# Projection om of a gated attention and mLSTM layer: eight block products, or seven by Strassen's identity

## The chip, the cores and the metric

The kernel runs on one core of one Trainium2 chip. The metric is the device time of one execution in microseconds; the median of several runs is given. The core has five engines with queues of their own: TensorE (PE in the profile, its weight loads PEld), VectorE (DVE), ScalarE (ACT), GpSimd (POOL) and SyncE (SP), which here issues most DMA transfers. They are ordered only by semaphores.

## The reference

One layer over 256 tokens of width 1024, in float32. A normalised and modulated h (256 x 1024) is multiplied by one wide weight matrix, and the product is cut into projections:

```python
h = _rmsnorm(x, norm_w) * (1 + scale) + shift          # scale, shift, gate from c @ w_ada
(qa, ka, va, za, qm, km, vm, zm, om, ig, fg, ga, gm) = jnp.split(h @ w_in, SPLIT_IDX, axis=-1)
ya = (attention(rmsnorm(qa), rmsnorm(ka), va) * silu(za)) @ w_att_proj
hm = mlstm(silu(conv(qm)), silu(conv(km)), vm, ig, fg)  # 4 heads of 256
hm = sigmoid(om) * hm
ym = (rmsnorm_per_head(hm) * silu(zm)) @ w_ml_proj
y = sigmoid(ga) * ya + sigmoid(gm) * ym
return x + gate * (y @ w_out)
```

Each of the wide projections is 256 x 1024 times 1024 x 1024. The change concerns `h @ w_in[:, om]`, of which only the sigmoid is used, and only in the mLSTM output.

## The kernel before, in words

**Precision.** Matrices are multiplied in a fast float32 form that keeps part of the mantissa. To keep float32 accuracy each operand is split into a high part and the rest, and a product takes three matmuls: high by high, high by rest, rest by high. h is split once into `hTh` and `hTl`, both transposed (8 k-tiles of 128 rows, 256 tokens). The weights are split as they pass: `split(g)` copies a weight group to `wh` on ACT (line 448) and subtracts to get `wl` on DVE (line 452; on POOL for the few groups in `pool_lo`).

**Groups.** After a first phase (modulation, and projections qa and ka by `mm_row`, line 198), the rest is a list of `chunks`, half a projection each, in a fixed order: va (three chunks), za, qm, km, att, zm, vm, om, ga, gm, ml, out (two each). A chunk of 512 output columns is four *groups*, each with two k-tiles of weights. The main loop runs over groups g. Projections of kind `tok` (zm, vm, om, out) hold tokens on the output partitions: per group 2 k-tiles x 2 token halves x 3 = 12 matmuls of 512 columns (lines 999 to 1001). Projections of kind `ws` hold the weights still: 24 matmuls of 256 columns (lines 1006 to 1009).

**The split ring.** `wh` and `wl` have five buffers (`HB = 5`). At step g the loop first issues `split(g + 4)`, which reuses the buffers of group g - 1; then, at the first group of a chunk, the evacuation of the chunk before (`EV`: `ev_vm` line 706, `ev_om` line 712, `ev_ga` line 718 and others); then the *hooks* of that step (`at(step, fn)`), an order of the other work written out by hand; then the group's matmuls. Every engine works its queue in this order.

**Weight loads.** SP loads weights in 1 MB pieces to six `raw` buffers (line 376): a piece holds two k-tiles of both halves of a projection, and `pump` issues the load six pieces on when a piece has been split for the last time. The weights of the modulation gate (`ada_gate`) come as four more 1 MB pieces ahead of the projections in `GSEG`, and are summed on DVE by `gate_acc` (line 832), two at a time, four and three groups ahead of that projection.

**PSUM.** Two large tiles `mm` (two banks each) alternate between chunks; four small tiles `aux` serve everything else.

**Around om.** With groups counted from va, zm is 44 to 51, vm 52 to 59, om 60 to 67, ga 68 to 75, gm 76 to 83, ml 84 to 91. `ml_scores` (lines 757 to 768) runs during zm and into vm. `ml_num` (lines 779 to 786) makes a head's nine matmuls, multiplies by sigmoid(om) on DVE (783) and sums squares on ACT; `ml_y` normalises two heads on DVE, POOL and DVE (line 805); `ml_T` transposes on PE (816) and splits the result (820, 821) for projection ml. For heads 0 and 1 these hang on the end of om's first half (steps 65, 66, 67, then 71, 72), for heads 2 and 3 on the end of its second half (69, 70, 71, then 75, 76).

**Slots.** Large tiles share tagged memory slots: a new tile in a slot waits for all accesses of the one before.

Of the kernel before, what the change touches and what calls it, by code (L numbers as in the profile page):

```python
# [9 lines left out]
F32 = mybir.dt.float32  # L10
# [5 lines left out]
D = 1024  # L16
# [50 lines left out]
def tile_hybrid(ctx: ExitStack, tc: tile.TileContext, x, c, params2, w_row, w_va, ada_mod, ada_gate,  # L67
# [304 lines left out]
    def mk_pair(src, c0, kp):  # L372
# [68 lines left out]
    def split(g, between=()):  # L441
        li, ks, cs = raw_of[g]
        w = rawt[li][:, ks, cs]
        n = chunks[g // 4]["n"]
        at0 = WS_AT if chunks[g // 4]["kind"] == "ws" else 0
        h = hl.tile([128, RING], F32R, name="wh", bufs=HB)[:, at0:at0 + 1024].rearrange("p (k n) -> p k n", k=2)[:, :, 0:n]
        l = hl.tile([128, RING], F32R, name="wl", bufs=HB)[:, at0:at0 + 1024].rearrange("p (k n) -> p k n", k=2)[:, :, 0:n]
        nc.scalar.copy(h, w)  # L448
# [3 lines left out]
        e.tensor_tensor(l, w, h.bitcast(F32), op=OP.subtract)  # L452
        whl[g] = (h, l)
# [252 lines left out]
        nc.scalar.copy(T["vm"][:, :, hs, 0:MD], v)  # L706
        nc.vector.tensor_tensor(T["vml"][:, :, hs], v, T["vm"][:, :, hs, 0:MD].bitcast(F32), op=OP.subtract)

    def ev_om(pt, half):
        if half == 0:  # L710
            T["om"] = slot("s2", [128, 2, D], F32, "omt")
        nc.scalar.activation(T["om"][:, :, half * 512:half * 512 + 512], pt, AF.Sigmoid)
# [135 lines left out]

    def gate_columns(kp):

        li, ks, cs = raw_of[4 * C["out", 1] + kp]
        w = rawt[li][:, ks, cs]
        nc.gpsimd.tensor_tensor(w, w, T["gateb"][:, cs].unsqueeze(1).to_broadcast([128, 2, 512]), op=OP.mult)

    def ev_out(pt, c0, n, t):
        cs = slice(c0, c0 + n)
        o = hl.tile([128, n], F32, name="o", tag="scr", bufs=2)
        if c0 < 512:
# [49 lines left out]
    at(4 * C["att", 0] - 10, gate_init)  # L908
    gate_left = {}
    for q, nm in enumerate(GSEG):  # L910
        s = 4 * C[nm, 0] - 4
        at(s, gate_acc, 2 * q)
        at(s + 1, gate_acc, 2 * q + 1)
        gate_left[s + 1] = gate_loads[q]
    at(4 * C["ga", 0], gate_write)
    at(4 * C["gm", 0] + 4, gate_read)
    for q in range(4):
        at(4 * C["ml", 0] + 3 + q, gate_columns, q)
    for hp in range(2):
# [28 lines left out]
        consumed.update(li for li in cons.get(g, []) if li not in gate_loads)  # L948
    pump()
    for g in range(NG):  # L950
        ci, kp = divmod(g, 4)
        ch = chunks[ci]
        if g + A < NG:
            split(g + A, hooks_between.get(g, []))
            consumed.update(li for li in cons.get(g + A, []) if li not in gate_loads)
        if kp == 0:
            if ci > 0:
                pc = chunks[ci - 1]
                if pc["name"] in EV and ci - 1 != C["za", 0]:
# [5 lines left out]
            if ci < NCH - 1:  # L965
# [12 lines left out]
        sh_, sl_ = (hTh, hTl) if ch["stat"] is None else (T[stat[ch["stat"]][0]], T[stat[ch["stat"]][1]])  # L978
        wh, wl = whl[g]
        if ci == NCH - 1:  # L980
            continue
        for kk in range(2):
            k = 2 * kp + kk
            first, last = k == 0, k == KT - 1
            if ch["name"] == "out":

                for i in (0, 1):
                    for t, c0 in ((0, 0), (0, 256), (1, 0), (1, 256)):
                        a = (sh_, sl_)[i][:, k, t * 128:(t + 1) * 128]
                        cs = slice(c0, c0 + 256)  # L990
                        for w in (wh, wl)[:2 - i]:
                            nc.tensor.matmul(mmt[ci][:, t, cs], a, w[:, kk, cs],  # L992
                                             start=first and i == 0 and c0 == 0 and w is wh,
                                             stop=last and i == 1 and c0 > 0, skip_group_check=True)
            elif ch["kind"] == "tok":
                for t in range(2):
                    a, b = sh_[:, k, t * 128:(t + 1) * 128], sl_[:, k, t * 128:(t + 1) * 128]
                    o = mmt[ci][:, t]
                    nc.tensor.matmul(o, a, wh[:, kk], start=first, stop=False)  # L999
                    nc.tensor.matmul(o, a, wl[:, kk], start=False, stop=False)  # L1000
                    nc.tensor.matmul(o, b, wh[:, kk], start=False, stop=last)  # L1001
            else:
                for i in range(4):
                    cs = slice(i * 128, (i + 1) * 128)
                    o = mmt[ci][:, i]
                    nc.tensor.matmul(o, wh[:, kk, cs], sh_[:, k], start=first and i % 2 == 0, stop=False,  # L1006
                                     skip_group_check=True)
                    nc.tensor.matmul(o, wh[:, kk, cs], sl_[:, k], start=False, stop=False, skip_group_check=True)  # L1008
                    nc.tensor.matmul(o, wl[:, kk, cs], sh_[:, k], start=False, stop=last and i % 2 == 1,  # L1009
                                     skip_group_check=True)  # L1010
    ci = NCH - 1
    for t, c0, n in ((0, 0, 512), (1, 0, 256), (1, 256, 256)):
        pt = ps.tile([128, n], F32, name="mm", bufs=2)
# [62 lines left out]
```

## Time and profile before

| | |
|---|---|
| median of 3 runs | 351.48 us (351.32, 351.48, 351.49) |
| profiled execution: first to last instruction (span) | 350.0 us |
| PE busy | 344.3 us, 98% |
| DVE, ACT, POOL busy | 247.0, 213.3, 87.8 us |
| DMA moved | 77.79 MB, mean 222 GB/s |
| TensorE clock granted | full |

The profiled execution is given by its span; the time of an execution on the device, as the runs list it, has some work around the span as well. Rows of a timeline read: start, duration, engine, line, operation, output <- inputs, shape, count, and in brackets how long the engine sat idle before and what released it. Rows of a group: line, engine, operation, count | busy us, mean ns | idle before and its releaser. The duration of a matmul contains its way through the array, so matmuls overlap: the distance of two starts is what counts. Rows of the windows give for each engine the busy time and, in brackets, the instructions.

### The profile page before, as it was taken

How to read it: one execution, taken by the hardware profiler on the slowest of the kernel's cores; microseconds unless marked ns; L12 is line 12 of the kernel's file. 1: busy time of each engine (PE TensorE's matmuls, PEld its weight loads, DVE VectorE, ACT ScalarE, POOL GpSimd, SP SyncE). 2: the span in 40 equal slices, each digit the busy share in tenths (PEclk: the TensorE clock that was granted, in tenths of full speed). 3: DMA queues.
4: the chain of work that ended last, by engine and by line, in shares of the span. 5: the costliest groups of instructions: out<-in, count | busy, mean ns of one | idle time of the engine just before them, and what ended most of it. 6: DMA issues, size and time to landing. Idle time of an engine off the chain costs nothing.

```text
span 350.0 us, 6175 instructions
## 1 busy us (share of the span) xinstructions
PE 344.3 (98%) x2432; PEld 323.1 (92%) x2432; DVE 247.0 (71%) x369; ACT 213.3 (61%) x331; POOL 87.8 (25%) x81
## 2 busy tenths in 40 slices
PE   8999999999999999999999999999999999999996
PEld 7788889999999999999998888888899999999995
DVE  4999996976994437768866693864475775469961
ACT  4768779799777867675646554445646374543510
POOL 4400002942202462555004352000010320452000
PEclk9999999999999999999999999999999999999999
DMA  7999999890671554493874837659119129291011
GB/s 286 416 413 416 415 419 418 223 385 13 197 285 62 161 200 134 151 375 125 322 279 151 330 120 245 237 163 388 51 29 381 72 70 367 107 292 69 2 62 60
DMA packets 23517, 77.79 MB, mean 222 GB/s; under 512 B 3001, under 2 KB 4929, under 8 KB 22849
## 3 DMA queue, kind: packets, MB, share of 16 engines
q1 hardware_dynamic: 23336, 76.87, 59.9%
q10 hardware_dynamic: 152, 0.53, 0.5%
q8 instruction: 19, 0.31, 0.3%
q14 instruction: 10, 0.07, 0.1%
HBM read 76.14 MB, written 1.25 MB: 221 GB/s over the span
## 4 chain that ended last, share of the span: by engine, by line
PE 96%; DMA 2%; DVE 1%; issue 0%; SPq 0%; ACT 0%; DVEq 0%; ACTq 0%
PE mm L1009 15%; PE mm L1006 15%; PE mm L1008 15%; PE pm L198 13%; PE mm L999 8%; PE mm L1000 8%; PE mm L1001 8%; PE mm L992 3%; DMA adat<-in_ada_mod_dram 2%; PE mm L1021 1%; PE aux L642 1%; PE mm L1020 1%; PE mm L1019 1%; PE aux L492 1%; PE aux L604 1%; PE aux L762 1%
## 5 line engine op out<-in xcount | busy, mean ns | idle before, releaser
L452 DVE TENSOR_TENSOR wl<-raw,wh 128x1024 fp32r<-128x1024 f32 (+1 forms) x92 | 118.7, 1302 | 64.1 <-ACT wh L448 64.1
L448 ACT CAST wh<-raw 128x1024 fp32r<-128x1024 f32 (+1 forms) x100 | 100.5, 1015 | 54.2 <-PE mm L1001 26.7
L1006 PE MATMUL mm<-hTh,wh 128*128 128x256 f32 x320 | 90.0, 281 | 0.0
L1008 PE MATMUL mm<-hTl,wh 128*128 128x256 f32 x320 | 88.7, 277 | 0.0
L1009 PE MATMUL mm<-hTh,wl 128*128 128x256 f32 x320 | 88.7, 277 | 0.0
L1006 PEld LDWEIGHTS mm<-hTh,wh 128*128 128x128 f32 x320 | 60.2, 188 | 0.0
L1008 PEld LDWEIGHTS mm<-hTl,wh 128*128 128x128 f32 x320 | 60.2, 188 | 0.0
L1009 PEld LDWEIGHTS mm<-hTh,wl 128*128 128x128 f32 x320 | 60.1, 188 | 0.0
L999 PE MATMUL mm<-wh,hTh 128*128 128x512 f32 (+1 forms) x144 | 53.0, 368 | 0.0
L1000 PE MATMUL mm<-wl,hTh 128*128 128x512 f32 (+1 forms) x144 | 52.6, 365 | 0.0
L1001 PE MATMUL mm<-wh,hTl 128*128 128x512 f32 (+1 forms) x144 | 52.6, 365 | 0.0
L1001 PEld LDWEIGHTS mm<-wh,hTl 128*128 128x128 f32 x144 | 27.0, 188 | 3.8
L999 PEld LDWEIGHTS mm<-wh,hTh 128*128 128x128 f32 x144 | 27.0, 188 | 3.6
L1000 PEld LDWEIGHTS mm<-wl,hTh 128*128 128x128 f32 x144 | 27.1, 188 | 3.5
L452 POOL TENSOR_TENSOR wl<-raw,wh 128x1024 fp32r<-128x1024 f32 x8 | 19.5, 2461 | 18.4 <-ACT wh L448 12.1
L183 ACT CAST wrh<-raw 128x512 fp32r<-128x512 f32 (+1 forms) x24 | 18.2, 761 | 8.0 <-DMA raw<-in_w_row_dram 7.9
L188 DVE TENSOR_TENSOR wrl<-raw,wrh 128x512 fp32r<-128x512 f32 (+1 forms) x26 | 20.3, 807 | 0.5 <-ACT wrh L183 0.5
L198 PE MATMUL pm<-wrh,hTh 128*128 128x512 f32 x64 | 19.9, 392 | 0.8 <-ACT hTh L168 0.8
L198 PE MATMUL pm<-wrh,hTl 128*128 128x512 f32 x64 | 19.8, 391 | 0.0
L198 PE MATMUL pm<-wrl,hTh 128*128 128x512 f32 x64 | 18.7, 391 | 0.0
L1009 PE MATMUL mm<-yah,wl 128*128 128x256 f32 x64 | 17.7, 276 | 0.0
L1006 PE MATMUL mm<-yah,wh 128*128 128x256 f32 x64 | 17.7, 276 | 0.0
(218 smaller groups left out, 659.3 us busy)
## 6 DMA issues: line engine op xcount, KB each, us to landing
raw<-in_w_in_dram SPq DMA_DIRECT2D x32, 1024.0 KB, 5.2
adat<-in_ada_mod_dram SPq DMA_DIRECT2D x16, 512.0 KB, 8.8
raw<-in_w_va_dram SPq DMA_DIRECT2D x6, 688.0 KB, 9.2
raw<-in_ada_gate_dram SPq DMA_DIRECT2D x4, 1024.0 KB, 6.8
raw<-in_w_att_proj_dram SPq DMA_DIRECT2D x4, 1024.0 KB, 4.8
raw<-in_w_ml_proj_dram SPq DMA_DIRECT2D x4, 1024.0 KB, 6.3
raw<-in_w_out_dram SPq DMA_DIRECT2D x4, 1024.0 KB, 6.3
raw<-in_w_row_dram SPq DMA_DIRECT2D x15, 256.0 KB, 8.1
```

What stands on the lines that cost most here:

```text
L183: copy(wsp[k][0][:, c0:c1], wrow[k][:, c0:c1])
L188: e.tensor_tensor(l[:, cs], wrow[k][:, cs], h[:, cs].bitcast(F32), op=OP.subtract)
L198: nc.tensor.matmul(pm[ch][:, t], a[:, k, t * 128:(t + 1) * 128], b[:, cs], start=k == 0 and i == 0, stop=k == KT - 1 and i == 2)
L448: nc.scalar.copy(h, w)
L452: e.tensor_tensor(l, w, h.bitcast(F32), op=OP.subtract)
L992: nc.tensor.matmul(mmt[ci][:, t, cs], a, w[:, kk, cs], start=first and i == 0 and c0 == 0 and w is wh, stop=last and i == 1 and c0 > 0, sk ...
L999: nc.tensor.matmul(o, a, wh[:, kk], start=first, stop=False)
L1000: nc.tensor.matmul(o, a, wl[:, kk], start=False, stop=False)
L1001: nc.tensor.matmul(o, b, wh[:, kk], start=False, stop=last)
L1006: nc.tensor.matmul(o, wh[:, kk, cs], sh_[:, k], start=first and i % 2 == 0, stop=False, skip_group_check=True)
L1008: nc.tensor.matmul(o, wh[:, kk, cs], sl_[:, k], start=False, stop=False, skip_group_check=True)
L1009: nc.tensor.matmul(o, wl[:, kk, cs], sh_[:, k], start=False, stop=last and i % 2 == 1, skip_group_check=True)
```

## The change

om is written as a 2 x 2 block product: tokens in two halves of 128, k in two halves of 512, columns in two halves of 512. Instead of eight block products, seven are made (`OM_PRODUCTS`, Strassen's identity in Winograd's form). A block product is a chunk of kind `sums` with two groups, each of 2 k-tiles x 3 = 6 matmuls of 512 columns, so om is 14 groups (60 to 73), ga starts at 74, gm at 82, ml at 90. Each product has a weight block of its own, a 1 MB load: three blocks of `w_in`, and four sums of blocks.

- The four sums of weight blocks are made in DRAM by eight DMAs that POOL issues, four plain copies and four that add, at steps 10, 15, ... 45.
- The four sums of blocks of h are made on DVE at steps 53 to 57 (`h_full`, `h_sum`), each split on ACT and DVE.
- The products go to four small `aux` tiles in place of the large ones. Products 0 and 2 use the first, 1 and 3 the second, 4 and 6 the third, 5 the fourth; the second of a pair is added to the first in PSUM after the first has been read. `ev_om(j)` runs at the first group after product j: on ACT for j = 0 and 2, on DVE for 1 and 3, on DVE and then a sigmoid on ACT for 4, 5, 6.
- `ml_num`, `ml_y` and `ml_T` of heads 0 and 1 hang on the end of om (75, 76, 77, then 81, 82), those of heads 2 and 3 three groups later (78, 79, 80, then 84, 85).
- The gate loads and `gate_acc` move one projection ahead (`GSEG`), since a slot that they use now holds a sum of h.

```diff
+OM_PRODUCTS = (((0, 0), 0), (1, 1), ((1, 0), 0), (2, 1), (0, 2), (3, 3), ((1, 1), 2))
+OM_FIRST = (0, 1, 4, 5)
+OM_SUMS = ((0, (0, 0), False), (2, (0, 1), False), (0, (0, 1), True), (2, (1, 1), True),
+           (1, 0, False), (1, (1, 1), True), (3, 1, False), (3, (1, 0), True))
+OM_SUM_AT = 10
...
-    seg("tok", win, COL["om"], "om")
+    for j, (blk, bank) in enumerate(OM_PRODUCTS):
+        chunks.append(dict(kind="sums", blk=blk, bank=bank, half=j, n=512, name="om", stat=None))
...
-    GSEG = ("att", "zm", "vm", "om")
+    GSEG = ("km", "att", "zm", "vm")
...
+    def om_sum(i, src, add):
+        dst = om_sums[i]
+        src = om_operand(src)
+        if add:
+            nc.gpsimd.dma_start(dst, src, accum_op=OP.add)
+        else:
+            nc.gpsimd.dma_start(dst, src)
+
+    def h_full():
+        T["hf"] = [hl.tile([128, 4, S], F32, name="hfull", tag="scr", bufs=2) for _ in range(2)]
+        T["om"] = slot("s2", [128, 2, D], F32, "omt")
+        for kh in range(2):
+            ks = slice(4 * kh, 4 * kh + 4)
+            nc.vector.tensor_tensor(T["hf"][kh], hTh[:, ks].bitcast(F32), hTl[:, ks].bitcast(F32), op=OP.add)
...
+    def h_sum(name):
...
+        nc.vector.tensor_tensor(f[:, i], x, y, op=op)
+        nc.scalar.copy(v[:, 0], f[:, i])
+        nc.vector.tensor_tensor(v[:, 1], f[:, i], v[:, 0].bitcast(F32), op=OP.subtract)
...
+    def ev_om(j):
...
+        if j == 0:
...
+            nc.scalar.mul(T["u"][:, 0], b[0], -1.0)
+        elif j == 1:
+            nc.vector.tensor_tensor(T["u"][:, 1], b[1], T["u"][:, 0], op=OP.add)
+        elif j == 2:
+            put(0, 0, b[0])
+        elif j == 3:
+            nc.vector.tensor_tensor(T["v"], b[1], T["u"][:, 0], op=OP.add)
+        elif j == 4:
+            nc.vector.tensor_tensor(part[1][1], T["v"], b[2], op=OP.subtract)
+            put(1, 1, part[1][1])
+        elif j == 5:
+            nc.vector.tensor_tensor(part[1][0], b[3], T["v"], op=OP.subtract)
+            put(1, 0, part[1][0])
+        else:
+            nc.vector.tensor_tensor(part[0][1], T["u"][:, 1], b[2], op=OP.subtract)
+            put(0, 1, part[0][1])
...
+    for q, (i, src, add) in enumerate(OM_SUMS):
+        at(OM_SUM_AT + 5 * q, om_sum, i, src, add)
+    s = start("vm") + 1
+    at(s, h_full)
+    for q, name in enumerate(("P5", "P6", "P3", "P7")):
+        at(s + 1 + q, h_sum, name)
     for hp in range(2):
-        s = done("om", hp)
+        s = done("om", 6) + 3 * hp
         at(s + 1, ml_num, 2 * hp)
         at(s + 2, ml_num, 2 * hp + 1)
         at(s + 3, ml_y, hp)
...
+            if ch["kind"] == "sums":
+                (a, b), o = om_stationary(ch["blk"]), T["ombank"][ch["bank"]]
+                fresh = ch["half"] == OM_FIRST[ch["bank"]]
+                nc.tensor.matmul(o, a[:, k], wh[:, kk], start=fresh and k == 0, stop=False, skip_group_check=True)
+                nc.tensor.matmul(o, a[:, k], wl[:, kk], start=False, stop=False, skip_group_check=True)
+                nc.tensor.matmul(o, b[:, k], wh[:, kk], start=False, stop=k == 3, skip_group_check=True)
```

More of the change, by code (lines that the diff above doesn't have):

```diff
@@ L343, in tile_hybrid, with start @@
     NCH = len(chunks)
-    NG = 4 * NCH
-    C = {}
+    C, G0, place = {}, [], []
     for i, ch in enumerate(chunks):
         C[ch["name"], ch["half"]] = i
+        G0.append(len(place))
+        place += [(i, kp) for kp in range(2 if ch["kind"] == "sums" else 4)]
+    NG = len(place)
+    G0.append(NG)
+    def start(name, half=0):
+        return G0[C[name, half]]
     def done(name, half):
-        return 4 * (C[name, half] + 1)
+        return G0[C[name, half] + 1]
     loads = []
@@ L378, in mk_pair, with om_block, om_operand, mk_block @@
         return f
+    om_sums = [dram.tile([128, 4, 512], F32, name=f"om_sum{i}") for i in range(4)]
+    def om_block(kh, nh):
+        c0 = COL["om"] + 512 * nh
+        return win[:, 4 * kh:4 * kh + 4, c0:c0 + 512]
+    def om_operand(blk):
+        return om_sums[blk] if isinstance(blk, int) else om_block(*blk)
+    def mk_block(blk):
+        def f():
+            v = raw_tile().rearrange("p (k n) -> p k n", k=4)
+            nc.sync.dma_start(v, om_operand(blk))
+            return v
+        return f
     NSINGLE = 3
-    GSEG = ("att", "zm", "vm", "om")
+    GSEG = ("km", "att", "zm", "vm")
     gate_loads = []
@@ L389, in tile_hybrid @@
                 last_use[li] = 4 * i + 2 * q + 1
+        elif ch["kind"] == "sums":
+            li = add_load(mk_block(ch["blk"]))
+            for kp in range(2):
+                raw_of[G0[i] + kp] = (li, slice(2 * kp, 2 * kp + 2), slice(0, 512))
+            last_use[li] = G0[i] + 1
         elif ch["half"] == 0:
@@ L395, in tile_hybrid @@
                 for hf in range(2):
-                    raw_of[4 * (i + hf) + kp] = (li, slice(0, 2), slice(hf * 512, hf * 512 + 512))
-                last_use[li] = 4 * (i + 1) + kp
+                    raw_of[G0[i + hf] + kp] = (li, slice(0, 2), slice(hf * 512, hf * 512 + 512))
+                last_use[li] = G0[i + 1] + kp
     xload = add_load(lambda: None)
@@ L443, in split @@
         w = rawt[li][:, ks, cs]
-        n = chunks[g // 4]["n"]
-        at0 = WS_AT if chunks[g // 4]["kind"] == "ws" else 0
+        n = chunks[place[g][0]]["n"]
+        at0 = WS_AT if chunks[place[g][0]]["kind"] == "ws" else 0
         h = hl.tile([128, RING], F32R, name="wh", bufs=HB)[:, at0:at0 + 1024].rearrange("p (k n) -> p k n", k=2)[:, :, 0:n]
@@ L707, in ev_vm @@
         nc.vector.tensor_tensor(T["vml"][:, :, hs], v, T["vm"][:, :, hs, 0:MD].bitcast(F32), op=OP.subtract)
[L709 to L712, printed above, removed]
+    def om_sum(i, src, add):
[5 more added lines that the diff above has]
+            nc.gpsimd.dma_start(dst, src)
@@ new lines, in h_full @@
+    def h_full():
[4 more added lines that the diff above has]
+            nc.vector.tensor_tensor(T["hf"][kh], hTh[:, ks].bitcast(F32), hTl[:, ks].bitcast(F32), op=OP.add)
+        T["A"] = {}
+    def h_sum(name):
+        a11, a21 = (T["hf"][0][:, :, t * 128:t * 128 + 128] for t in range(2))
+        a12, a22 = (T["hf"][1][:, :, t * 128:t * 128 + 128] for t in range(2))
+        f = T["om"].rearrange("p t (n k s) -> p (t n) k s", n=2, k=4)
+        i, x, y, op = dict(P5=(0, a22, a21, OP.subtract), P6=(1, f[:, 0], a11, OP.add),
+                           P3=(2, f[:, 1], a12, OP.subtract), P7=(3, a21, a11, OP.subtract))[name]
+        if i % 2 == 0:
+            T["S", i // 2] = slot(("s3", "bias")[i // 2], [128, 2, 2, 4, 128], F32R, "hsum")
+        v = T["S", i // 2][:, i % 2]
+        nc.vector.tensor_tensor(f[:, i], x, y, op=op)
+        nc.scalar.copy(v[:, 0], f[:, i])
+        nc.vector.tensor_tensor(v[:, 1], f[:, i], v[:, 0].bitcast(F32), op=OP.subtract)
+        T["A"][name] = v[:, 0], v[:, 1]
@@ new lines, in om_stationary, with put @@
+    def om_stationary(blk):
+        plain = {(0, 0): (0, 0), (1, 0): (0, 1), 3: (1, 1)}
+        if blk in plain:
+            t, kh = plain[blk]
+            ks, ts = slice(4 * kh, 4 * kh + 4), slice(t * 128, t * 128 + 128)
+            return hTh[:, ks, ts], hTl[:, ks, ts]
+        return T["A"][{0: "P5", 1: "P6", 2: "P7", (1, 1): "P3"}[blk]]
+    def ev_om(j):
+        om, b = T["om"], T["ombank"]
+        part = [[om[:, t, 512 * n:512 * n + 512] for n in range(2)] for t in range(2)]
+        def put(t, n, src):
+            nc.scalar.activation(part[t][n], src, AF.Sigmoid)
+        if j == 0:
+            T["u"] = hl.tile([128, 2, 512], F32, name="omu", tag="scr", bufs=2)
+            T["v"] = hl.tile([128, 2, 512], F32, name="omv", tag="scr", bufs=2)[:, 0]
+            nc.scalar.mul(T["u"][:, 0], b[0], -1.0)
[14 more added lines that the diff above has]
+            put(0, 1, part[0][1])
@@ L849, in gate_columns @@
     def gate_columns(kp):
-        li, ks, cs = raw_of[4 * C["out", 1] + kp]
+        li, ks, cs = raw_of[start("out", 1) + kp]
         w = rawt[li][:, ks, cs]
@@ L864, in tile_hybrid @@
     EV = dict(va=ev_va, za=ev_za, att=ev_att,
-              zm=ev_zm, vm=ev_vm, om=ev_om, ga=ev_ga, gm=ev_gm, ml=ev_ml)
+              zm=ev_zm, vm=ev_vm, ga=ev_ga, gm=ev_gm, ml=ev_ml)
     at(0, q_scale)
@@ L902, in tile_hybrid @@
         at(done("za", 1) + 1 + q, att_av, 4 + 2 * q)
-    s = 4 * C["zm", 0]
+    s = start("zm")
     for half in range(2):
@@ L907, in tile_hybrid @@
         at(s + 5 * half + 4, ml_scores, 2 * half + 1)
-    at(4 * C["att", 0] - 10, gate_init)
+    at(start(GSEG[0]) - 10, gate_init)
     gate_left = {}
     for q, nm in enumerate(GSEG):
-        s = 4 * C[nm, 0] - 4
+        s = start(nm) - 4
         at(s, gate_acc, 2 * q)
@@ L914, in tile_hybrid @@
         gate_left[s + 1] = gate_loads[q]
-    at(4 * C["ga", 0], gate_write)
-    at(4 * C["gm", 0] + 4, gate_read)
+    at(start("ga"), gate_write)
+    at(start("gm") + 4, gate_read)
     for q in range(4):
-        at(4 * C["ml", 0] + 3 + q, gate_columns, q)
+        at(start("ml") + 3 + q, gate_columns, q)
+    for q, (i, src, add) in enumerate(OM_SUMS):
[4 more added lines that the diff above has]
+        at(s + 1 + q, h_sum, name)
     for hp in range(2):
-        s = done("om", hp)
+        s = done("om", 6) + 3 * hp
         at(s + 1, ml_num, 2 * hp)
@@ L950, in tile_hybrid @@
     for g in range(NG):
-        ci, kp = divmod(g, 4)
+        ci, kp = place[g]
         ch = chunks[ci]
@@ L958, in tile_hybrid @@
                 pc = chunks[ci - 1]
-                if pc["name"] in EV and ci - 1 != C["za", 0]:
+                if pc["kind"] == "sums":
+                    ev_om(pc["half"])
+                elif pc["name"] in EV and ci - 1 != C["za", 0]:
                     EV[pc["name"]](mmt[ci - 1], pc["half"])
@@ L964, in tile_hybrid @@
             sh = [128, 2, 512] if ch["kind"] == "tok" else [128, 4, 256]
-            if ci < NCH - 1:
+            if ch["kind"] == "sums":
+                if ch["half"] == 0:
+                    T["ombank"] = []
+                if ch["bank"] == len(T["ombank"]):
+                    T["ombank"].append(aux([128, 512]))
+            elif ci < NCH - 1:
                 mmt[ci] = ps.tile(sh, F32, name="mm", bufs=2)
@@ L984, in tile_hybrid @@
             first, last = k == 0, k == KT - 1
-            if ch["name"] == "out":
+            if ch["kind"] == "sums":
+                (a, b), o = om_stationary(ch["blk"]), T["ombank"][ch["bank"]]
[3 more added lines that the diff above has]
+                nc.tensor.matmul(o, b[:, k], wh[:, kk], start=False, stop=k == 3, skip_group_check=True)
+            elif ch["name"] == "out":
                 for i in (0, 1):
@@ L1016, in tile_hybrid @@
             for c1 in range(0, n, 256):
-                wh, wl = (w[:, k % 2, c0 + c1:c0 + c1 + 256] for w in whl[4 * ci + k // 2])
+                wh, wl = (w[:, k % 2, c0 + c1:c0 + c1 + 256] for w in whl[G0[ci] + k // 2])
                 o = pt[:, c1:c1 + 256]
```

## The prediction

> **What bounds the kernel now.** I read the page's busy times, clock and chain first, then the windows of the stages around projection om, then each engine's timeline inside them.
>
> ```profile
> span 350.0 us, 6175 instructions
> PE 344.3 (98%) x2432; PEld 323.1 (92%) x2432; DVE 247.0 (71%) x369; ACT 213.3 (61%) x331; POOL 87.8 (25%) x81
> PEclk9999999999999999999999999999999999999999
> PE 96%; DMA 2%; DVE 1%; issue 0%; SPq 0%; ACT 0%; DVEq 0%; ACTq 0%
> ```
>
> ```profile
> core 0: us, PE busy (x) PEld busy (x) DVE busy (x) ACT busy (x) POOL busy (x), PEclk, DMA share, GB/s
> 212.00:231.06 19.06, 19.06 (x86) 15.77 (x85) 12.41 (x13) 7.88 (x9) 1.16 (x2) 1.00 0.70 248
> 231.06:252.80 21.74, 21.74 (x106) 18.35 (x105) 11.04 (x12) 12.50 (x23) 0.00 (x0) 1.00 0.58 205
> 252.80:275.00 22.20, 22.20 (x183) 21.81 (x182) 13.77 (x25) 10.86 (x23) 5.20 (x7) 1.00 0.52 190
> ```
>
> TensorE is the bound: 98% busy, 96% of the chain, full clock. Windows: groups 53 to 59 (vm), about the om stage, ga. In each PE never idles, while DVE works 65%, 51% and 62% and ACT 41%, 57% and 49%. So a matmul less is time saved, as long as ACT and DVE keep ahead. How far they are ahead:
>
> ```profile
> start us, us, engine line op out<-in xcount [idle before <-releaser]
> 236.50 0.39 PE L999 MATMUL mm<-wh,hTh 128*128 128x512 f32 x1
> ...
> 239.22 0.39 PE L999 MATMUL mm<-wh,hTh 128*128 128x512 f32 x1
> ```
>
> ```profile
> 220.43 1.05 ACT L448 CAST wh<-raw 128x1024 fp32r<-128x1024 f32 x1 [1.66 <-PE mm L1001]
> 221.39 1.01 ACT L706 CAST vaug<-mm 128x1024 fp32r<-128x1024 f32 x1
> ...
> 236.70 1.05 ACT L448 CAST wh<-raw 128x1024 fp32r<-128x1024 f32 x1 [1.67 <-PE mm L1001]
> ...
> 243.21 1.28 ACT L712 ACT_TABLE_LOAD   x1
> ```
>
> ```profile
> 221.51 1.23 DVE L452 TENSOR_TENSOR wl<-raw,wh 128x1024 fp32r<-128x1024 f32 x1 [1.49 <-ACT wh L448]
> 222.66 1.22 DVE L707 TENSOR_TENSOR vml<-mm,vaug 128x1024 fp32r<-128x1024 f32 x1
> ...
> 237.79 1.22 DVE L452 TENSOR_TENSOR wl<-raw,wh 128x1024 fp32r<-128x1024 f32 x1 [1.50 <-ACT wh L448]
> ```
>
> A group of twelve 512-wide matmuls runs from 236.50 to 239.22: 2.72 us, 0.2267 us each. The split of the group four ahead can't start sooner: its cast waits for PE's last read of the ring buffer (released by PE, 0.20 after the group start), DVE follows 1.09 later, and the split is done 2.5 us after the group started. It frees ACT after 0.96 us (220.43 to 221.39) and DVE after 1.15 (221.51 to 222.66).
>
> **The change, part by part.**
>
> *Matmuls.* om goes from 2 x 8 x 2 x 3 = 96 to 7 x 4 x 3 = 84, all 512 wide: 12 x 0.2267 = **-2.72 us**, if nothing waits. But a group is now six matmuls, 1.36 us, and there are 14 splits for 8. The lead of four groups shrinks from 10.9 to 5.4 us, of which the split takes 2.5.
>
> *Sums of h.* Steps 53 to 57 (vm) get on DVE two 128x1024 additions (1.15 each), eight 128x512 operations and on ACT four 512-wide casts; two gate accumulations leave.
>
> ```profile
> L832 DVE CUSTOM_DVE_ANT_0 raw<-raw,cbg,prm 128x1024 f32<-128x1024 f32 x8 | 11.4, 1419 | 0.0
> L734 DVE TENSOR_TENSOR yf<-mm,gmt 128x512 f32<-128x512 f32 x4 | 2.7, 682 | 0.0
> L736 ACT CAST yh<-yf 128x512 fp32r<-128x512 f32 x4 | 2.5, 622 | 8.8 <-DVE yf L735 8.8
> ```
>
> At 0.62 of DVE time each (0.68 less the overlap of 0.07 seen above): +2.3 +5.0 -2.4 = +4.9 us, against some 6.6 idle in the vm window; in amount it fits. In order it fits less well: each sum goes DVE, ACT, DVE, and the next cast queues behind ACT's copy, which waits for DVE, which waits for the split. One step of this loop is 1.09 + 1.15 + 0.75 + 0.57 = 3.56 us against PE's 2.72, for four steps, with ev_vm's 1.0 in one of them. Steps 58 and 59 win back 1.8 each. Carried through step by step, the split of group 64 ends at 235.0 on this clock; without the sums it would at 233.6. Lead remains, so PE reaches om at 231.06 as before.
>
> *Om itself.* The evacuations of products 1 and 4 must be read on DVE before products 3 and 6 may add to the same PSUM tile, one product (2.72 us) later, and DVE has a split ahead of them. Even with no lag, that read ends at 2.44 + 0.72 = 3.16 after the product starts: 0.44 us of wait, twice. With the lag carried: product 2 may start at 236.85 (ACT's copy of product 0; 0.35 late); the split of group 68 frees DVE at 240.7, the read of product 1 ends at 241.41, and product 3, due at 239.57, waits **1.84**; product 6, due at 249.57, waits for the read of product 4 until 250.19, **0.62**. Sum +2.81. In between, the splits of groups 65, 67, 70, 72 and 74 end at 237.3, 239.6, 243.7, 246.7 and 249.6, while PE reaches them at 238.2, 242.8, 246.9, 250.2 and 252.9: the data are never what PE waits for, the PSUM tiles are. ACT's table load (1.28, one as before, now at product 2) falls in product 3 and eats only lead. om ends at 252.91; 96 matmuls would have ended at 252.82. So the stage returns what it saves: -2.72 + 2.81 = **+0.09**.
>
> *ga.* All four ml_num and both ml_y now come after om, the two halves three groups apart instead of four, behind splits that ACT and DVE finish late.
>
> ```profile
> 247.64 0.75 DVE L783 TENSOR_TENSOR omt<-aux,omt 128x256 f32<-128x256 f32 x2
> ...
> 257.29 1.68 DVE L805 SCALAR_TENSOR_TENSOR omt<-omt,f,zmt 128x256 f32<-128x256 f32 x4 [1.71 <-POOL f L800]
> ...
> 272.21 3.79 DVE L805 SCALAR_TENSOR_TENSOR omt<-omt,f,zmt 128x256 f32<-128x256 f32 x4 [1.70 <-POOL f L800]
> ```
>
> ```profile
> 272.12 2.40 POOL L719 TENSOR_TENSOR gat<-gat,attT 128x1024 f32<-128x1024 f32 x1
> ...
> 301.95 6.37 POOL L853 TENSOR_TENSOR raw<-raw,gateb 128x1024 f32<-128x1024 f32 x2 [14.08 <-DMA gateb<-gd]
> ```
>
> ```profile
> 304.19 1.86 DVE L452 TENSOR_TENSOR wl<-raw,wh 128x1024 fp32r<-128x1024 f32 x1 [1.49 <-ACT wh L448]
> ```
>
> ```profile
> 277.79 0.44 PE aux L816 x4
> ...
> 324.95 10.88 PE mm L992 x96
> ```
>
> In om's last three products ACT's sigmoid waits for DVE's read, and the next cast stands behind it; so DVE ends its part of step 74 (split 78, read of product 6) at 259.4, 6.5 us after that group started. A step with ml_num takes it 3.6 (split 1.15 behind the cast, product 0.75, then ACT's sums before the next cast); one with ml_y 7.0 (the split, four small operations, POOL's power 1.7, four products 1.6). Steps 75 to 80 make 26.7 us, so the last ml_y ends at 286.2. PE (2.72 a group, a head's nine matmuls 1.02 at 10.88/96, a transpose step 0.44) comes to the third transpose step at 285.2 and waits **1.0**, where it ran through at 277.79 before. The second ml_num finds its PSUM tile read late: **0.18**. The first product of POOL with ga (2.40) now lies beside a split on this path. Beside POOL work DVE's rows lengthen: the split of 1.22 to 1.86, the four products of 1.68 to 3.79. So 0 to 2.1; I take the split's, its own kind: **+0.64**.
>
> The Trainium skill, SBUF — State Buffer, § Who interferes with whom, says why: a VectorE instruction with two SBUF inputs contends with a GpSimd instruction that reads SBUF, and the loser waits for the whole instruction. By a full lock of 2.40 the sum would be 1.8 higher; 1.86 against 1.22 bears out a part of it, 3.79 nearly all.
>
> *Weight sums.* Eight DRAM to DRAM transfers of 1 MB, issued by POOL at steps 10 to 45, four of them adding; and seven 1 MB loads for om instead of four.
>
> ```profile
> GB/s 286 416 413 416 415 419 418 223 385 13 197 285 62 161 200 134 151 375 125 322 279 151 330 120 245 237 163 388 51 29 381 72 70 367 107 292 69 2 62 60
> raw<-in_w_in_dram SPq DMA_DIRECT2D x32, 1024.0 KB, 5.2
> ```
>
> ```profile
> SPq L376 <- DVE wl L452: 147.4, 32, 17.4
> ```
>
> SP waits for buffers, not for data; a load is issued six groups (16.3 us) before its split and lands in 5.2, which leaves 8 to 11 us. From 88 to 188 us the DMA moves about 190 of the 415 GB/s it reached early: room for some 20 MB, the sums need 8 written and more read. No row shows a DMA issued by POOL or one that adds: from 0 up to 6 us (an add that holds loads back 10 us in two of the four places beyond that cover). I take 0, by the 5.2. On POOL (25% busy) each issue costs between SP's third of a microsecond and a 2.5 us operation; its splits in qm and km are made four groups (10.9 us) ahead, so 0. The two chained waits at steps 35 and 40 have 13.6 us each; behind them on POOL stand splits and the k halves of ml_split. Om's loads start ten groups early: 0.
>
> *Gate accumulations* run one segment earlier, first at steps 24 and 25 beside conv.
>
> ```profile
> 154.61 1.37 DVE L832 CUSTOM_DVE_ANT_0 raw<-raw,cbg,prm 128x1024 f32<-128x1024 f32 x1
> ```
>
> ```profile
> 154.00:176.00 22.00, 22.00 (x197) 22.00 (x196) 19.45 (x33) 14.19 (x20) 6.11 (x3) 1.00 0.69 248
> ```
>
> The same pair beside km's conv left PE at 22.00 of 22.00: 0. The earlier load takes a buffer one step; the same cover hides it. ACT's read of c waits for the last attention scores, as its exponential before it does: 0. ga's slot still holds SD until the last ml_num: ACT's ga evacuation waits about a group, with sums and a cast behind it, but ACT is by then later than that: 0.
>
> Sum: -2.72 + 2.81 + 0.18 + 1.00 + 0.64 = **+1.9 us**: a span of 351.9 for 350.0. The runs' median 351.48 lies 1.48 above the profiled span; 351.48 + 1.9 = **353.4**.
>
> **The rivals.**
> *A, the lead holds (faster).* The sums of h fall into DVE's idle time, om starts unlagged, and only the two waits of 0.44 remain: -2.72 + 0.88 = -1.8, 349.6; with no wait 348.8. For: 6.6 us idle in vm, PE never starved now. Against: the loop of 3.56 us and 14 splits at 1.15 plus evacuations, 19.7 us of DVE for 19.0 of PE. It decides at the split of group 64: done before about 233.6, A wins.
> *B, the transfers show.* An add of 1 MB that slows loads past their 8 to 11 us of cover stalls PE between 110 and 190 us; +3 to +6 on the forecast, 356 to 359. Against: the free half of the bandwidth. The Trainium skill, SBUF — State Buffer, in the box on VectorE blocking DMA, adds that descriptors of a GpSimd-issued DMA wait while VectorE holds the shared port; no run yet shows it.
> *C, POOL's full lock* in ga: 1.8 more, 355.2.
> *D, half the lag*: waits of about 2.7 in all, no change, 351.5. The change then does nothing to the time.
>
> **How the numbers follow.** Forecast 0.36, A 0.29, D 0.19, C 0.08, B 0.08. About 0.2% (0.7 us) is what runs of this kernel can tell from no change. Faster is A, same is D, slower the rest: 0.29, 0.19, 0.52. The range runs from A's 349.4 into B's beginning, 356.5, leaving out about 0.15; the forecast's own is 352.2 to 355.
>
> **What would show it.** Right: in om gaps of PE ahead of products 3 and 6 released by DVE reads; wl ending 1 to 2 us late at group 64; a PE wait for omt ahead of the third transpose step in ga; PE busy about 2.7 less. Wrong: PE without gaps in om (A), gaps for wl or loads before 200 us (B), or DVE not waiting for ACT's casts in vm.

## The result, and the profile after

The changed kernel takes 354.74 us (median of 4 runs, 354.62 to 355.22) against 351.45; the ratio is 1.0091, 95% interval 1.0077 to 1.0106. It is slower by 3.3 us, where 1.9 were forecast.

The page of the changed kernel, its busy times, clock, POOL's DMA queue and chain:

```profile
span 353.4 us, 6216 instructions
PE 344.1 (97%) x2420; PEld 320.2 (91%) x2420; DVE 268.3 (76%) x390; ACT 220.5 (62%) x344; POOL 101.3 (29%) x89
PEclk9999999999999999999999999999999999999999
q0 software_dynamic: 2720, 8.39, 10.5%
PE 69%; DVE 13%; issue 10%; ACT 5%; POOL 3%; ACTq 0%; POOLq 0%; DVEq 0%
```

The twelve matmuls are gone (2420 for 2432), the clock is full, and the chain, 96% PE before, runs through DVE, ACT and POOL for a fifth of the span. The windows of om, ga, gm and out:

```profile
core 0: us, PE busy (x) PEld busy (x) DVE busy (x) ACT busy (x) POOL busy (x), PEclk, DMA share, GB/s
231.41:253.87 22.46, 19.93 (x85) 15.54 (x84) 19.85 (x20) 18.45 (x20) 0.00 (x0) 1.00 0.93 325
253.87:281.64 27.77, 27.49 (x237) 27.29 (x236) 17.58 (x26) 12.18 (x30) 3.97 (x4) 1.00 0.47 153
281.64:305.53 23.89, 23.18 (x203) 22.82 (x202) 15.71 (x26) 14.86 (x25) 3.94 (x4) 1.00 0.48 171
327.29:350.02 22.73, 22.29 (x194) 21.89 (x192) 15.19 (x19) 6.31 (x8) 0.00 (x0) 1.00 0.11 42
```

PE is short of work in each. What it waits for, in its own timeline (the bracket names the releaser):

```profile
191.76 0.86 PE L855 MATMUL aux<-qms,kms 128*128 128x256 f32 x5 [0.34 <-POOL qms L843]
...
237.42 0.50 PE L1094 MATMUL aux<-wh,hTh 128*128 128x512 f32 x1 [0.41 <-ACT omu L790]
242.03 0.50 PE L1094 MATMUL aux<-wh,hsum 128*128 128x512 f32 x1 [1.59 <-DVE omu L792]
251.03 0.47 PE L1094 MATMUL aux<-wh,hsum 128*128 128x512 f32 x1 [0.53 <-DVE omt L798]
...
278.05 0.66 PE L909 MATMUL aux<-ident,omt 128*128 128x128 f32 x4 [0.28 <-ACT den L877]
287.65 0.30 PE L909 MATMUL aux<-ident,omt 128*128 128x128 f32 x1 [0.31 <-DVE omt L898]
288.35 0.55 PE L909 MATMUL aux<-ident,omt 128*128 128x128 f32 x3 [0.40 <-DVE omt L898]
...
333.25 0.39 PE L1104 MATMUL mm<-wh,yh 128*128 128x256 f32 x1 [0.35 <-ACT yh L829]
```

Three waits in om are for the reads of products 0, 1 and 4, as forecast. A row's idle time counts from the modelled end of the matmul before; by starts the cost is higher, since in a full stream a matmul starts 0.16 us before the last one ends. So I count each stage from its first matmul to the next stage's, and out to the start of its last matmul. The table gives these lengths for all kernels below; "front" is from the first va matmul to om. The phase ahead of va is left out: it is the same code in all, and va starts anywhere from 54.8 to 56.1 us.

| kernel | front | om | ga | gm | ml | out | together |
|---|---|---|---|---|---|---|---|
| before | 175.44 | 23.94 | 26.17 | 21.85 | 21.77 | 21.64 | 290.81 |
| before, ml_num moved (e8) | 175.44 | 21.75 | 27.28 | 22.97 | 21.76 | 21.73 | 290.93 |
| changed | 176.04 | 22.46 | 27.77 | 23.89 | 21.76 | 22.73 | 294.65 |
| e1 no weight sums | 175.44 | 22.47 | 27.85 | 23.79 | 21.76 | 22.87 | 294.18 |
| e2 own PSUM tiles | 175.44 | 19.07 | 32.56 | 23.58 | 22.61 | 21.72 | 294.98 |
| e3 sigmoids later | 175.44 | 22.45 | 27.28 | 22.97 | 21.76 | 21.73 | 291.63 |
| e4 sums of h spread | 175.55 | 21.08 | 27.80 | 24.51 | 22.61 | 21.71 | 293.26 |
| e5 = e2 + e3 + e4 | 175.44 | 19.04 | 27.28 | 22.97 | 21.76 | 21.73 | 288.22 |
| e6 no gate columns | 175.44 | 22.47 | 27.79 | 23.89 | 21.76 | 21.65 | 293.00 |
| e7 = e5 + ga evacuated later | 175.44 | 19.04 | 27.28 | 23.20 | 21.76 | 22.79 | 289.51 |
| e9 = e7 + ACT sums later | 175.44 | 19.04 | 27.27 | 22.97 | 21.76 | 21.65 | 288.13 |
| e10 = e9 without e7's edit | 175.44 | 19.04 | 27.27 | 22.98 | 21.75 | 21.65 | 288.13 |
| e11 = e9 without e2's edit | 175.44 | 21.06 | 27.28 | 22.97 | 21.76 | 21.65 | 290.16 |

Against e8, which has the same hooks in the same stages, the changed kernel loses 0.60 ahead of om, 0.71 in om, 0.49 in ga, 0.92 in gm and 1.00 in out: 3.72. The profiled execution of the changed kernel is the slowest of its four, 0.5 us above their median, so the lengths add up to more than the 3.3 us between the medians.

### The profile page after: what moved, and what is told of

It is laid out like the page before. It is cut to its first block, busy times and chain, and to the rows that moved or that the text cites. A ratio compares the mean times of both kernels' runs of the same rounds, so it can differ in the third digit from the quotient of the medians.

```text
span 353.4 us, 6216 instructions
## 1 busy us (share of the span) xinstructions
PE 344.1 (97%) x2420; PEld 320.2 (91%) x2420; DVE 268.3 (76%) x390; ACT 220.5 (62%) x344; POOL 101.3 (29%) x89
## 3 DMA queue, kind: packets, MB, share of 16 engines
q1 hardware_dynamic: 24408, 80.02, 61.2%
q0 software_dynamic: 2720, 8.39, 10.5%
## 4 chain that ended last, share of the span: by engine, by line
PE 69%; DVE 13%; issue 10%; ACT 5%; POOL 3%; ACTq 0%; POOLq 0%; DVEq 0%
PE pm L203 13%; PE mm L1120 8%; PE mm L1118 8%; PE mm L1121 8%; DVE wl L485 7%; PE mm L1113 5%; PE mm L1111 5%; PE mm L1112 5%; ACT wh L481 3%; PE mm L1104 1%; DVE kmT L715 1%; DVE omt L898 1%; PE xps L268 1%; PE aux L675 1%; PE mm L1133 1%
## 5 line engine op out<-in xcount | busy, mean ns | idle before, releaser
L485 DVE TENSOR_TENSOR wl<-raw,wh 128x1024 fp32r<-128x1024 f32 (+1 forms) x98 | 128.3, 1333 | 46.6 <-ACT wh L481 46.4
L481 ACT CAST wh<-raw 128x1024 fp32r<-128x1024 f32 (+1 forms) x106 | 105.1, 1016 | 27.6 <-DMA raw<-in_w_in_dram 11.3
L1111 PE MATMUL mm<-wh,hTh 128*128 128x512 f32 (+1 forms) x112 | 40.6, 362 | 0.0
L1112 PE MATMUL mm<-wl,hTh 128*128 128x512 f32 (+1 forms) x112 | 40.2, 359 | 0.0
L1113 PE MATMUL mm<-wh,hTl 128*128 128x512 f32 (+1 forms) x112 | 40.2, 359 | 0.0
L485 POOL TENSOR_TENSOR wl<-raw,wh 128x1024 fp32r<-128x1024 f32 x8 | 20.5, 2573 | 16.7 <-ACT wh L481 16.7
L1113 PEld LDWEIGHTS mm<-wh,hTl 128*128 128x128 f32 x112 | 21.0, 188 | 2.5
L1111 PEld LDWEIGHTS mm<-wh,hTh 128*128 128x128 f32 x112 | 21.1, 188 | 2.4
L1112 PEld LDWEIGHTS mm<-wl,hTh 128*128 128x128 f32 x112 | 21.1, 188 | 2.4
L1121 PE MATMUL mm<-ymh,wl 128*128 128x256 f32 x64 | 17.7, 276 | 0.0
```

## The experiments

Three theories. Theory 1: the order of DVE and ACT work makes the loss, in om and in what follows. Theory 2: DVE has too little time for 14 splits, in any order. Theory 3: the DRAM transfers hold up the loads.

**e1, no weight sums.** The loads of products 1, 3, 4 and 5 fetch plain blocks; this kernel leaves the sums of weights out.

```diff
-        return om_sums[blk] if isinstance(blk, int) else om_block(*blk)
+        return om_block(blk // 2, blk % 2) if isinstance(blk, int) else om_block(*blk)
...
-    for q, (i, src, add) in enumerate(OM_SUMS):
-        at(OM_SUM_AT + 5 * q, om_sum, i, src, add)
```

> The changed kernel without the eight DRAM to DRAM transfers; the four products that used a sum load a plain weight block instead, so the sums of weights are left out and everything else stays. Theory 1 (the loss is made by the order of DVE and ACT work in om and after it: PSUM tiles read late 3.0 us, lag in ga and gm 1.5, out 1.1): only the 0.35 us ahead of om go, about 354.3 us, and om keeps its three PE waits of 0.4, 1.6 and 0.5. Theory 2 (DVE has too little time for 14 splits, whatever the order): the same 354.3. Theory 3 (the transfers hold up the loads, and what is late later starts there): 352.5 or less, and PE's waits in om shrink.

354.87 us, ratio 1.0101 (1.0089 to 1.0114): as the changed kernel. Front falls by 0.60 to the length before, om keeps its three waits, so theory 3 can claim no more than that 0.60, and by the medians nothing. In the changed kernel the loads were in fact late. Its waits (sum, count, longest, in us), and then its DMA issues (the last number is the median from issue to landing):

```profile
ACT wh L481 <- DMA raw<-in_w_in_dram: 11.3, 5, 4.6
```

```profile
raw<-in_w_in_dram SPq DMA_DIRECT2D x31, 1024.0 KB, 7.4
om_sum<-in_w_in_dram POOLq DMA_DIRECT2D x6, 1024.0 KB, 10.0
```

Five casts waited 11.3 us for these loads, 4.6 at the longest, and one waited 1.8 for a load of `w_att_proj`; behind va none waits for a load in the kernel before or in e1. The lead of four groups took nearly all of it: only ACT's cast of q, which stands behind a late cast and which POOL's split of q needs, came through to PE, at 191.76. The other kernels that keep the transfers show a front of 175.44 to 175.55 with casts as late (4.6 us in e9), so the 0.60 is not there in every execution.

**e2, own PSUM tiles.** Product order 0, 1, 4, 2, 3, 5, 6 (by their numbers in the changed kernel), product 6 in a fifth tile, one more DVE subtraction.

```diff
-OM_PRODUCTS = (((0, 0), 0), (1, 1), ((1, 0), 0), (2, 1), (0, 2), (3, 3), ((1, 1), 2))
+OM_PRODUCTS = (((0, 0), 0), (1, 1), (0, 2), ((1, 0), 0), (2, 1), (3, 3), ((1, 1), 4))
...
```

> The changed kernel with the products in another order and five PSUM tiles, so that no product adds to a tile that was read less than two products before; one more 512-wide DVE subtraction. Theory 1: the PE waits of 0.4, 1.6 and 0.5 us in om are gone, with their restarts 3.0 us, and a part comes back as lag in ga: 352.0 to 353.0 us. Theory 2: PE waits for splits (wl) instead, and om is as long as before: 354.2 to 354.9. Theory 3: as theory 2.

355.21 us, ratio 1.0112 (1.0099 to 1.0126). My expectation missed. om runs at PE's pace, 19.07 us, with no wait; and all of it, and more, is lost from ga on. ga holds one wait, of the transposes:

```profile
277.12 0.65 PE L910 MATMUL aux<-ident,omt 128*128 128x128 f32 x4 [3.46 <-ACT den L878]
```

That wait is not the whole of ga's 4.8 us over the changed kernel. Soon after it the granted clock falls to half for 3.4 us, which costs some 1.7 (an estimate, half of the 3.4). The window from the end of the wait to gm has a mean clock of 0.67:

```profile
277.12:282.32 5.20, 5.20 (x32) 5.20 (x33) 1.97 (x4) 3.57 (x13) 0.00 (x0) 0.67 0.00 0
```

Another execution of e2, with a mean clock of 1.00, took 354.80, so the clock alone does not make its time. ml is 0.85 longer as well, without a wait: its matmuls start 0.1178 us apart in place of 0.1133, from the first to the last. What sets this pace no run shows. Taking away a wait of PE only let PE run further ahead of DVE and ACT. Alone, this looked like theory 2.

**e3, sigmoids one group later.** The sigmoids after products 4, 5 and 6 are issued behind the next group's cast.

```diff
...
-            put(1, 1, part[1][1])
+            put_later(1, 1, part[1][1])
...
+        while late:
+            fn, a = late.pop()
+            fn(*a)
         if kp == 0:
             if ci > 0:
                 pc = chunks[ci - 1]
```

> The changed kernel with the three sigmoids that follow a DVE subtraction issued one group later on ACT, behind the next cast. Theory 1: ACT no longer sits 2.0 us three times with a cast behind it; the waits in om stay, those in ga and gm (1.5) and the out stage (1.1) shrink by half or more: 352.8 to 353.8 us. Theory 2 and theory 3: 354.5 to 354.9, since DVE's amount of work is the same.

351.97 us, ratio 1.0018 (1.0009 to 1.0027), more than expected: with the same instructions, 2.8 us less than the changed kernel by the medians. om is unchanged; ga, gm and out are back to e8's lengths, which is 2.4 us. ACT's timeline at the three sigmoids, in the changed kernel and then in e3:

```profile
250.92 0.63 ACT L785 ACTIVATE omt<-omt 128x512 f32<-128x512 f32 x1 [2.04 <-DVE omt L798]
251.46 1.98 ACT L481 CAST wh<-raw 128x1024 fp32r<-128x1024 f32 x2
255.52 0.63 ACT L785 ACTIVATE omt<-omt 128x512 f32<-128x512 f32 x1 [2.08 <-DVE omt L801]
256.05 1.98 ACT L481 CAST wh<-raw 128x1024 fp32r<-128x1024 f32 x2
260.11 0.63 ACT L785 ACTIVATE omt<-omt 128x512 f32<-128x512 f32 x1 [2.08 <-DVE omt L804]
```

```profile
249.87 0.63 ACT L786 ACTIVATE omt<-omt 128x512 f32<-128x512 f32 x1 [0.69 <-DVE omt L802]
...
253.33 0.63 ACT L786 ACTIVATE omt<-omt 128x512 f32<-128x512 f32 x1 [0.59 <-DVE omt L805]
...
256.79 0.63 ACT L786 ACTIVATE omt<-omt 128x512 f32<-128x512 f32 x1
```

The sigmoid waited 2 us for DVE, which waited for a split, which waited for a cast; the next casts stood behind the sigmoid. Counted from om's first matmul, the last sigmoid starts 2.3 us earlier in e3 (26.4 for 28.7).

**e4, sums of h spread.** First operation, ACT copy and DVE remainder in three steps.

```diff
...
         at(s + 1 + q, h_sum, name)
+        at(s + 2 + q, h_cast, name)
+        at(s + 3 + q, h_low, name)
```

> The changed kernel with each sum of h spread over three groups (first operation, ACT copy a group later, DVE remainder another later), so that no cast waits for DVE. Theory 1: om starts with DVE less than 1 us behind in place of 5, the wait ahead of product 3 falls from 1.6 to about 0.5, 353.4 to 354.2 us. Theory 2: the same work, so 354.5 to 354.9. Theory 3: 354.7.

353.77 us, ratio 1.0066 (1.0050 to 1.0083), as theory 1 had it. om falls to 21.08; the wait for product 0's read is gone, the others are 0.56 and 0.92. ga and gm keep their waits and take 0.65 more, and ml takes 0.85 more: most of gm and all of ml run at the slower pace seen in e2, with no wait. So the time understates what the edit saves in om, 1.4 us.

**e5, the three edits together.**

> The three edits together: own PSUM tiles and order, sigmoids one group later, sums of h spread over three groups. Theory 1 (order of DVE and ACT work): om runs without a PE wait (19.1 us) and ACT enters ga on time, so the saving of 2.7 us is kept but for the lag made in ga: 349.5 to 350.8 us, below the kernel before. Theory 2 (DVE has too little time): 351.0 to 352.0, what om saves turns up as PE waits in ga, as it did with the PSUM edit alone.

349.17 us, ratio 0.9934 (0.9921 to 0.9947): faster than before, a little below theory 1's range. om 19.04, everything behind it as in e8. Theory 2 falls: DVE has the same or more to do, and nothing is lost.

**e8, the move alone.** The kernel before, with `s = done("om", 1) + 3 * hp` for ml_num, ml_y and ml_T.

> The kernel before, with the one edit that heads 0 and 1 of ml_num, ml_y and ml_T come after the whole of om, and heads 2 and 3 three groups later, as in the changed kernel. om keeps its 96 matmuls. Theory 1: DVE and ACT enter ga on time and four ml_num in a row cost PE little: 351.3 to 351.9 us; the loss in ga of the changed kernel comes from the lag it enters with. Rival (the crowding in ga alone makes that loss): 352.4 to 353.5.

351.62 us, ratio 1.0005 (0.9996 to 1.0014). Four ml_num in a row cost PE 0.12 us by the table. The loss in ga and gm is made by the lag that DVE and ACT bring from om.

**e7 and e9: ga's evacuation later, ACT's sums later.**

```diff
+        if hp:
+            at(s + 2, lambda: ev_ga(mmt[C["ga", 0]], 0))
...
```

```diff
...
+        at(s + 2, ml_sums, 2 * hp)
         at(s + 2, ml_num, 2 * hp + 1)
+        at(s + 3, ml_sums, 2 * hp + 1)
```

> The same three edits, and the first evacuation of ga issued behind the last ml_num, whose reads its memory slot waits for. Theory 1: ACT no longer stands some 4 us ahead of that evacuation with casts and ml_num's sums behind it; ga and gm shorten by up to 1 us more: 349.0 to 350.3 us. Rival (ACT would have waited for DVE there anyway): within 0.3 us of the kernel with three edits.

> The same four edits, and ACT's sums of ml_num one group later, behind the next cast. Theory 1: the loop of cast, split, product, ACT sums, next cast in ga (1.6 us of ACT waiting each of four times) is opened, and PE waits nowhere after om: 348.6 to 349.6 us. Rival (the loop is no longer than PE's own step of 3.7 us, so it costs nothing): as the kernel with four edits.

e7: 350.28 us, ratio 0.9968 (0.9957 to 0.9979). The time lies in the range, but not for the reason given: against e5, ga didn't shorten, gm and out grew by 0.23 and 1.06 (for out, see e6). The rival, within 0.3 us of e5, fails too. e9: 348.36 us (348.27 to 348.47), ratio 0.9913 (0.9900 to 0.9927), the fastest, a little below its range. The page of e9 and its window of om:

```profile
span 346.4 us, 6220 instructions
PE 341.6 (99%) x2420; PEld 320.7 (93%) x2420; DVE 264.1 (76%) x391; ACT 221.6 (64%) x344; POOL 99.6 (29%) x89
```

```profile
230.27:249.31 19.04, 19.04 (x86) 15.77 (x85) 17.07 (x18) 15.59 (x17) 0.00 (x0) 1.00 0.83 297
```

PE never stops from va to the end. 288.13 against 290.81 is 2.68 us, twelve matmuls at 0.2267 being 2.72. In om DVE works 17.07 of 19.04 us: it is short of slack, not of time. The rest of the 3.0 us between the medians is not explained by the edits: in the profiled executions va starts 0.8 us earlier in e9 than before, after code that is the same in both.

**e10, e9 without e7's edit.**

> The kernel with five edits but for one: the first evacuation of ga stands again ahead of the last ml_num. Theory 1: the place of that evacuation matters little once ACT's sums come a group later; 348.2 to 348.9 us. Rival (ACT's wait of 4 us for the slot reaches PE): 349.3 to 350.3.

348.93 us, ratio 0.9918 (0.9902 to 0.9935), a shade above theory 1's range, and the same stage lengths as e9; its va starts 0.8 us later. The place of ga's evacuation costs PE nothing once the sums come later.

**e11, e9 with the four tiles of the changed kernel.**

> The kernel with five edits but for one: the order of the products and the four PSUM tiles are those of the changed kernel again. Theory 1: the PE waits ahead of products 3 and 6 come back at 0.5 to 0.9 us each with their restarts, om is 20.5 to 21.1 us, and nothing of it is lost again later: 349.9 to 350.6 us. Theory 2 (DVE's time, not the tiles): 348.3 to 348.8, as with five tiles.

350.79 us, ratio 0.9975 (0.9962 to 0.9987), a shade above the range. om is 21.06, 2.02 more than e9, and every other stage the same. So the two waits for PSUM reads, with no other lag about, cost 2.0 us:

```profile
240.44 0.50 PE L1119 MATMUL aux<-wh,hsum 128*128 128x512 f32 x1 [0.56 <-DVE omu L803]
...
249.82 0.47 PE L1119 MATMUL aux<-wh,hsum 128*128 128x512 f32 x1 [0.90 <-DVE omt L809]
```

**e6, no gate columns.** The changed kernel without POOL's four products of w_out with the gate; the second half of its output lacks the gate.

```diff
-    for q in range(4):
-        at(start("ml") + 3 + q, gate_columns, q)
```

> The changed kernel without POOL's four multiplications of w_out by the gate (gate_columns); the second half of the output lacks the gate. Theory 1: the out stage loses its 1.1 us, since DVE's splits for out no longer alternate with POOL's products (four splits took 12.9 us); om, ga and gm stay as they are: 353.5 to 354.0 us. Rival (DVE is late in the out stage because it enters ml late, not because of POOL): 354.5 to 354.9, the out stage stays at 22.7.

353.49 us, ratio 1.0060 (1.0036 to 1.0083), as theory 1 had it. out falls from 22.73 to 21.65; om, ga and gm stay. POOL and DVE in the changed kernel, then DVE in e6:

```profile
308.78 12.42 POOL L946 TENSOR_TENSOR raw<-raw,gateb 128x1024 f32<-128x1024 f32 x4 [13.58 <-DMA gateb<-gd]
```

```profile
309.42 12.87 DVE L485 TENSOR_TENSOR wl<-raw,wh 128x1024 fp32r<-128x1024 f32 x4 [0.54 <-ACT wh L481]
322.21 0.68 DVE L827 TENSOR_TENSOR yf<-mm,gmt 128x512 f32<-128x512 f32 x1
```

```profile
314.08 1.22 DVE L485 TENSOR_TENSOR wl<-raw,wh 128x1024 fp32r<-128x1024 f32 x1 [1.49 <-ACT wh L481]
316.80 1.23 DVE L485 TENSOR_TENSOR wl<-raw,wh 128x1024 fp32r<-128x1024 f32 x1 [1.50 <-ACT wh L481]
317.94 0.68 DVE L827 TENSOR_TENSOR yf<-mm,gmt 128x512 f32<-128x512 f32 x1
```

Four splits take 12.87 us in place of 1.22 each, in step with POOL; the evacuation of ml's first half (L827) stands behind them. Before, the four products were spread from 302 to 317 us, and two of them began in gaps of DVE. In the changed kernel SP's read of the gate came at 301.0, not 292.4, behind loads that waited for late splits; so POOL began late and met DVE in full. Counted from the first matmul of ml:

| kernel | SP reads the gate | POOL's first product | ml's first evacuation | out |
|---|---|---|---|---|
| before | -10.7 | -1.1 | 15.2 | 21.64 |
| e5 | -6.6 | 1.5 | 15.7 | 21.73 |
| changed | -4.5 | 3.3 | 16.7 | 22.73 |
| e7 | -4.5 | 3.4 | 16.8 | 22.79 |

e7 has no lag from om and loses the same, so om's lag is one way to make the gate late and not the only one. In e4 that evacuation begins 16.4 us into ml, but ml is 0.85 longer there, which fits its out of 21.71.

## Why the prediction was right or wrong, point by point

**The direction and the main mechanism held.** Strassen's twelve matmuls are worth 2.7 us (e9), and the order of DVE and ACT ate them. PE's waits in om came where the hand schedule had them: 0.35, 1.84 and 0.62 forecast, 0.41, 1.59 and 0.53 as idle time. The read of product 1 was forecast to start at 240.7 on the clock of before and started at 241.29, with om itself 0.35 late. The lag came from the sums of h, as laid out: the splits beside them start 3.45, 3.47, 4.59 and 3.47 us apart, forecast 3.56, and 4.56 with ev_vm. The last of three in the bottom row, the split of group 64, ends at 235.7, or 235.4 on the clock of before, forecast 235.0:

```profile
217.23 1.21 DVE L485 TENSOR_TENSOR wl<-raw,wh 128x1024 fp32r<-128x1024 f32 x1
...
220.68 1.23 DVE L485 TENSOR_TENSOR wl<-raw,wh 128x1024 fp32r<-128x1024 f32 x1 [0.26 <-ACT wh L481]
...
224.15 1.23 DVE L485 TENSOR_TENSOR wl<-raw,wh 128x1024 fp32r<-128x1024 f32 x1 [0.26 <-ACT wh L481]
...
228.74 1.22 DVE L485 TENSOR_TENSOR wl<-raw,wh 128x1024 fp32r<-128x1024 f32 x1 [0.26 <-ACT wh L481]
...
232.21 3.50 DVE L485 TENSOR_TENSOR wl<-raw,wh 128x1024 fp32r<-128x1024 f32 x3 [0.26 <-ACT wh L481]
```

One sign did not come: PE's busy time fell by 0.2 us and not by 2.7. A stopped stream counts as busy for longer: in om PE is busy 19.93 us with the matmuls that take 19.04 in e9, whose page has the 2.7 less (341.6 for 344.3).

**Om was mis-sized.** 2.81 of waiting were forecast; om took 22.46 us for 19.04 of matmuls, 3.42. The idle times sum to 2.53, the rest is what a stopped stream of matmuls loses beside them: the starts either side of the three waits lie 0.80, 1.98 and 0.91 apart for 0.23, which is 3.0, and 0.4 is spread. The smallest wait, 0.44 each without any lag, was too small as well: e11 has 2.02 for two.

**ga and gm: right in place, the size in part by luck.** 1.82 forecast, 1.41 measured against e8. PE did wait for omt at the third transpose step, 0.31 and 0.40. The second ml_num cost no wait; 0.28 at the first transposes, for ACT's sums, stands in its place. The stretch beside POOL hit ml_y's first products, 3.80 us for 1.67, and not a split: the 2.1 that the prediction gave as its upper bound, where it took 0.64.

```profile
272.52 3.80 DVE L898 SCALAR_TENSOR_TENSOR omt<-omt,f,zmt 128x256 f32<-128x256 f32 x4 [1.73 <-POOL f L893]
...
287.02 1.67 DVE L898 SCALAR_TENSOR_TENSOR omt<-omt,f,zmt 128x256 f32<-128x256 f32 x4 [1.70 <-POOL f L893]
```

So the last ml_y ended at 288.3 on the clock of before, where 286.8 were forecast (286.2 and the 0.64); but PE came to the third step at 287.0, where 285.2 were forecast, and so waited less. The two misses offset each other.

By the Trainium skill, SBUF — State Buffer, § Who interferes with whom, the loser of a VectorE instruction with two SBUF inputs and a GpSimd one that reads SBUF waits for the whole instruction. The rows come near it: 12.87 us for four splits of 1.22 leave 2.0 of waiting each, beside products that take POOL 2.4 where DVE is idle.

**Out was left out.** The schedule stopped at ml with DVE caught up. It did not follow SP: the gate's read is queued behind loads, loads wait for splits, and the products on POOL wait for the gate. That step was passed over, a term put at nothing that measured 1.0 us (e6). The queues followed were those of ACT, DVE and POOL, not SP's.

**Front: rival B in small.** Loads were late at six casts, by up to 4.6 us. The cover of 8 to 11 us, taken from the row of 5.2, was too kind: beside the transfers loads took 7.4 in the median, at a DMA share of 0.91 from 160 to 210 us, 0.65 before. (The prediction read 190 GB/s for the kernel before from 88 to 188 us; the window gives 205, and room for 21 MB all the same.) Yet the lead of the split held but for 0.60.

**A step whose reason was wrong.** I held that ACT would reach ga's evacuation too late to wait for its slot. It waited 2.60:

```profile
272.40 1.03 ACT L811 ACTIVATE gat<-mm 128x1024 f32<-128x1024 f32 x1 [2.60 <-PE aux L874]
```

e10 against e9 shows that PE does not feel it there, with ACT's sums issued later. No run moves it alone in the changed kernel, so there the zero is not shown, and its reason was wrong.

**Rival A** fails as the kernel stands, and wins when the loops are opened (e5, e9). It was said to be decided at the split of group 64, which was late as forecast; but the sigmoids, 2.4 us behind om by e3, decide more than the sums of h, 1.4 in om by e4. The hand schedule held both, but priced ga's lag without asking which edit would remove it.

## What to carry to other kernels

When a change makes the bound engine's work shorter, lay out the helpers' queues in order: a helper that waits for another helper, with the next piece of the ring queued behind it, makes a loop whose length is the sum of both. Issue the waiting half one step later; here three sigmoids moved by one group were worth 2.4 us and no instruction less. And follow a lag to the end of the kernel, through the DMA queue too, and test edits together: the own PSUM tiles were worth nothing alone and 2.0 us once the lag was gone.

## What the runs showed of the hardware

Plain and adding DRAM to DRAM transfers of 1 MB from POOL hold POOL for 0.55 to 1.21 us each. Their queue moved 8.39 MB in 10.5% of the span of 16 engines, 226 GB/s, where the loads' queue moved 80.02 MB in 61.2%, 370 GB/s. The plain ones landed after 5.5 to 7.7 us and the adding ones after 8.7 to 12.8, while loads went from 5.2 to 7.4 in the median.

In e2 a wait of PE of 3.46 us was followed by 3.4 us at half of the full clock. The 192 matmuls of ml, of 256 columns each, start 0.1133 us apart in eleven kernels and 0.1178 in e2 and e4, without a wait and with a granted clock of 1.00; no run shows why.
